# A two-layer hybrid decoder step on one core: another order of features in the output projections, row scores behind a merge, and later norms

## The chip, the core and the metric

The kernel runs on one core of one Trainium2 chip. The core has a matrix engine (TensorE; PE in the profile, its weight loads are PEld), a vector engine (VectorE, DVE), an activation engine (ScalarE, ACT), a general engine (GpSimd, POOL) and SyncE (SP), which issues the DMAs. SBUF is the on-chip memory, PSUM holds what matmuls sum up. The metric is the device time of one execution in microseconds.

## The reference: what is computed

One inference step of a trunk with two layers, for a prompt of 1024 tokens and 8 sample streams of 8 tokens each, 1024 features wide, in float32:

```python
for l in range(DEPTH):                                   # 2 layers
    if l < N_A_LAYERS:                                   # layer 0
        q, k, v, gate, qm = retention_inputs(xp, w_in_a[l], pos_p)
        o, st = retention_prompt(q, k, v, log_g)
        mix_p = concatenate([retention_output(o, gate), memory_attention(qm, mkv_p)])
    else:                                                # layer 1
        for g, (window, _) in enumerate(DIL_PAIRS):      # (128,1) (512,4) (2048,16)
            o, lse = dilated_prompt(q_p[:, :, hs], kv_p[:, :, 0, hs], kv_p[:, :, 1, hs], window, dil)
        mix_p = concatenate([combine_groups(outs_p, lses_p), memory_attention(qm_p, mkv_p)])
    xp = deepnorm_residual(xp, mix_p @ w_out[l], ln_mix_g[l], ln_mix_b[l])
    xp = deepnorm_residual(xp, swiglu_ffn(xp, w_ffn_in[l], w_ffn_out[l]), ln_ffn_g[l], ln_ffn_b[l])
```

The sample tokens go through the same layers, with retention states and key/value caches as inputs. `deepnorm_residual(x, h)` is the layer norm of `ALPHA * x + h`. `combine_groups` weighs the outputs of the three window groups by the softmax of their log-sums.

## The kernel before

**Layout.** Features lie on the 128 partitions, in 8 tiles of 128 (`KT`); the 1088 tokens (1024 of the prompt, 64 of the samples) lie along the free axis. They go in three chunks, `CH` = columns 0 to 512, 512 to 768 and 768 to 1088; the last holds the samples. `xh` and `xl` are the residual stream split in two fp32r halves; `mx` is what a mixer computes and later the sum that is normed. A float32 product is three matmuls, `wl*xh`, `wh*xl`, `wh*xh` (L316 to L318, and L764 to L766 and L814 to L816 in the FFN). The weight halves are made on the way: ACT rounds `wh`, DVE or POOL subtracts `wl` (L149, L152; these two lines are helpers that record most copies and elementwise operations).

**Order of the work.** A main program issues the projections. Small jobs (attention of a tile, a merge, a norm) are generators in a queue (`Streams`). At certain places of a projection the main program calls `S.tick()`, and each active job takes a step: up to `S.window` jobs, `S.rate` steps per tick. A job's `yield n` keeps it back for n ticks, a `yield` of a condition until that holds (`wait`). `S.until(cond)` takes steps, with ticks but no projection, until the condition holds. Within a dense product the ticks come after the features in `S.at`: of `TK`, (1, 3, 5) for block 0 of the second output projection, (4,) for the other blocks of either. Behind all this, a planner of the framework lays out each engine's queue: what was issued earlier has priority, but an instruction whose operands and buffers are there can be placed ahead of an earlier one that is not ready. So the issue order is a wish, and the trace shows what became of it.

**Layer 0** (`layer_a`, about 60 to 510 us): six retention heads, each with projections V, K, Q and a gate; the gates of heads 4 and 5 come last (`LATE`). `retention` is a job of some steps per head and chunk; its last transposes are the tile `rot` (L1078), which wait for `on` (L1063), which needs the statistics of L1055.

**Layer 1** (`layer_b`, about 1390 to 1785 us): six units (window group, half of the heads), `UNITS = ((2,0), (1,0), (0,0), (2,1), (1,1), (0,1))`. Each projects V, K, Q and then adds jobs to the queue. For the groups 1 and 2 these are `row_scores` (scores of the sample queries against cached keys, on DVE: 16 steps, each with one or two loads of `kc`, one of `qb`, one multiply, L1419, and two sums, L1422), `caches`, eight `attend`, a `spill`, and `sample`, which needs the rows and holds a lock (`locked`) for the length of its run, so that the samples of the units go one after another. For group 0 there is a `local_chunk` per chunk, which attends and then merges the three groups into `mx` (transposes of `fe`, tile `mtr`, L1353) and sets `("merge", j, c)`; then `sample`, and `merge_sample(j)`, which needs the three samples of j and sets `("msamp", j)` (tile `smt`, L1503). The rows of the units run one after another too (key `"rows"`). Before the change rows(1,1) run from about 1723 to 1787 us.

**Output projection** (`out_proj`, both layers): `mix = mx @ w_out`. Block 0 is chunk 0, block 1 is chunks 1 and 2. For each of the 8 features, `mx` is split into halves and `mx` gets the residual back (`xh + xl`). The halves of the first two features of block 0, and of all of block 1, lie in slots; those of later features of block 0 overwrite `xh` and `xl` of features whose residual was already returned. Then for each of 8 columns `m` the product over k = 0 to 7 goes to a PSUM bank (`dbank`: pool `pd` with 3 banks; `bank`: 4 banks), and DVE adds it to `ALPHA * mx` (L692). Block 1 of layer 1 waits for all merges, `("caches", 0, j)` and `("msamp", j)`.

**Norms** (`norm`): sums over the features, a matmul with `onesinv` for the mean (`lnm`, L599), subtraction, squares, a matmul for the variance (`lnv`, L619), its root on POOL (`lnr`), a matmul that spreads it (`lnb`, L630), and scale and shift. `LNY` gives the ticks before `lnm`, between `lnm` and `lnv`, and between `lnv` and `lnb`: the first triple for chunk 0 after the mixer, the second for the `calm` norms (chunks 1 and 2 after the mixer, chunk 0 after the FFN), the third for chunks 1 and 2 after the FFN. A calm norm first stands back by `LAZY` ticks, as do the outputs of chunk 0 in the last block (`y_out`). `combine_x` makes the inputs of the FFN from the normed chunks; the FFN's block 0 needs chunk 0, its block 1 the others.

**FFN** (`ffn`): two blocks of 512 and 576 tokens, 22 tiles of the hidden width in 6 groups; a tile is seven products (each 12 matmuls, then a tick), and after a group the output weights are applied.

Of the kernel before, what the change touches and what calls it, by code (L numbers as in the profile page):

```python
# [9 lines left out]
F32R = mybir.dt.float32r  # L10
# [4 lines left out]
P = 128  # L15
D = 1024
KT = 8
# [70 lines left out]
def trunk(ctx: ExitStack, tc: tile.TileContext, A: dict, O: dict, g128, g8):  # L88
# [13 lines left out]
    mm = nc.tensor.matmul  # L102
    dma = nc.sync.dma_start
    S = Streams(3)
    LNY = ((1, 5, 2), (3, 11, 5), (4, 7, 2))
    LAZY = (14, 14)
    RT = (2.3, 3.0, 1.0, 4.25, 4.25, 2.5)
    LAST = (((1,), (2,)), ((2,), (1,)))
    TK = ((3,), (2, 5), (1, 3, 5), (4,))
# [8 lines left out]
    def wait(*keys):  # L118
        if not all(k in done for k in keys):
            yield lambda: all(k in done for k in keys)  # L120
# [9 lines left out]
    def slot(shape, dt=F32, name="slot"):  # L130
        return slots.tile(shape, dt, tag="slot", name=name)
# [4 lines left out]
    def bank(name="bank"):  # L136
        return pa.tile([P, 512], F32, tag="pa", name=name)

    def dbank(name="pd"):
        return pd.tile([P, 512], F32, tag="pd", name=name)  # L140
# [10 lines left out]
    def tt(out, a, b, op, eng=None):  # L151
        (eng or nc.vector).tensor_tensor(out=out, in0=a, in1=b, op=op)  # L152
# [147 lines left out]
    def weights(key, ahead=None, keep=False):  # L300

        assert plan[at["next"]][0] == key, (plan[at["next"]][0], key)
        at["next"] += 1
        if not keep:
            for w in held:
                w.clear()
            held.clear()
        held.append([piece(1), piece(PA[1] if ahead is None else ahead)])
        return held[-1]

    def dense(out, w, rhs, kt=KT):

        for k in range(kt):
            rh, rl = rhs(k)
            wh, wl = (t[:, k % 4, :] for t in w[k // 4])
            mm(out, lhsT=wl, rhs=rh, start=(k == 0), stop=False)  # L316
            mm(out, lhsT=wh, rhs=rl, start=False, stop=False)  # L317
            mm(out, lhsT=wh, rhs=rh, start=False, stop=(k == kt - 1))  # L318
            if k in S.at and kt == KT:
                S.tick()  # L320
# [340 lines left out]
    BLK = (((0, 512),), ((512, 256), (768, 320)))  # L661
    BCH = ((0,), (1, 2))

    def out_proj(l, ready):
        for blk in range(2):
            S.at = TK[2] if l and blk == 0 else TK[3]
            S.until(lambda: all(k in done for c in BCH[blk] for k in ready(c)), blk if l else 1)
            b0, bn = BLK[blk][0][0], sum(n for _, n in BLK[blk])
            bs = slice(b0, b0 + bn)
            parts = []  # L670
            for k in range(KT):
                if blk == 0 and k > 1:
                    h, lo = xh[:, k - 2, bs], xl[:, k - 2, bs]
                elif k % 2 == 0:
                    hs, ls = (slot([P, 2, bn], F32R, nm) for nm in ("mixh", "mixl"))
                    h, lo = hs[:, 0], ls[:, 0]
                else:
                    h, lo = hs[:, 1], ls[:, 1]
                acopy(h, mx[:, k, bs])
                tt(lo, mx[:, k, bs], h.bitcast(F32), ALU.subtract)  # L680
                parts.append((h, lo))
                tt(mx[:, k, bs], xhf[:, k, bs], xlf[:, k, bs], ALU.add, nc.gpsimd if blk else nc.vector)
            done.add(("moved", l, blk))
            sums = [None, None]
            for m in range(KT):
                w = weights(("wo", l, blk, m))
                for i, c in enumerate(BCH[blk]):
                    c0, n = CH[c]
                    ps = (bank("po") if blk and m % 2 else dbank())[:, :n]
                    dense(ps, w, lambda k: tuple(t[:, c0 - b0:c0 - b0 + n] for t in parts[k]))  # L690
                    y = mx[:, m, c0:c0 + n]
                    nc.vector.scalar_tensor_tensor(out=y, in0=y, scalar=ALPHA, in1=ps, op0=ALU.mult, op1=ALU.add)  # L692
                    if blk == 0:
                        sums[i] = stat_add(sums[i], m, c, nc.vector)
                    S.tick()
            for i, c in enumerate(BCH[blk]):
                S.add(norm(c, sums[i], 0, l), level=2)
            S.add(combine_x(l, blk), level=2)
# [465 lines left out]
    def layer_b():  # L1164
# [219 lines left out]
        def row_scores(gi, j, Qt):  # L1384
# [30 lines left out]
            nxt = load(0)  # L1415
            for i in range(16):
                (kc, qb), nxt = nxt, load(i + 1) if i < 15 else None
                yield SR[i % 2]
                tt(qb, qb, bc(kc, 2, [P, 2, 2, P]), ALU.mult)  # L1419
                b, hf = i // 2, slice(i % 2 * 2, i % 2 * 2 + 2)  # L1420
                for h in range(2):
                    nc.vector.tensor_reduce(out=s5[:, hf, b, h, :], in_=qb[:, :, :, h * 64:(h + 1) * 64], op=ALU.add, axis=AX.X)  # L1422
# [141 lines left out]
    S.add(locked(mem_sample(0)))  # L1564
    layer_a()
    S.rate = RT[2]
    out_proj(0, lambda c: [("ret", h, c) for h in range(NRH)] + [("memT", 0, T) for T in range(8)] + [("mems", 0)])
    ffn(0, background)
    S.until(lambda: ("ln", 1, 0, 1) in done and ("ln", 1, 0, 2) in done and ("xparts", 0) in done)
    S.rate, S.at, S.window = RT[3], TK[1], WIN_[0]  # L1570
    layer_b()
    S.rate, S.window = RT[4], WIN_[1]
    out_proj(1, lambda c: [("merge", j, c) for j in range(2)] + [k for j in range(2) for k in (("caches", 0, j), ("msamp", j)) if c == 2])
    S.rate, S.window = RT[5], 3
    ffn(1, background)
    S.until(lambda: not S.q)
# [99 lines left out]
```

## Time and profile before

| what | time |
| --- | --- |
| median of 3 runs | 2707.31 us (2706.66 to 2708.17) |
| the profiled execution | 2703.15 us |
| its span, first to last instruction | 2701.3 us |
| PE busy in it | 2606.2 us |
| DVE, ACT, POOL busy | 1821.3, 1200.6, 933.4 us |
| mean granted clock of TensorE | 0.990 |

The profile is of one execution, and its times add up to that execution's time, not to the median. Busy times are unions of the instructions of an engine; PE's instructions are pipelined, so a busy PE need not be at its peak. In a timeline row stand the start, the length, the engine, the line, the operation, out<-in with the program's names, the shapes and the count, and in brackets how long the engine was idle before it and which instruction's end released it. In a view of stages each engine has its busy time and in brackets its count of instructions, then come the granted clock, the share of the DMA engines' time, and the rate in GB/s.

### The profile page before, as it was taken

How to read it: one execution, taken by the hardware profiler on the slowest of the kernel's cores; microseconds unless marked ns; L12 is line 12 of the kernel's file. 1: busy time of each engine (PE TensorE's matmuls, PEld its weight loads, DVE VectorE, ACT ScalarE, POOL GpSimd, SP SyncE). 2: the span in 40 equal slices, each digit the busy share in tenths (PEclk: the TensorE clock that was granted, in tenths of full speed). 3: DMA queues.
4: the chain of work that ended last, by engine and by line, in shares of the span. 5: the costliest groups of instructions: out<-in, count | busy, mean ns of one | idle time of the engine just before them, and what ended most of it. 6: DMA issues, size and time to landing. Idle time of an engine off the chain costs nothing. (4 is left out here: it accounts for less than half of the span.)

```text
span 2701.3 us, 48271 instructions
## 1 busy us (share of the span) xinstructions
PE 2606.2 (96%) x18057; PEld 2360.9 (87%) x18057; DVE 1821.3 (67%) x3843; ACT 1200.6 (44%) x2617; POOL 933.4 (35%) x1118
## 2 busy tenths in 40 slices
PE   8999999999999999999999999989999999999997
PEld 8778888798999989999977777768989998899997
DVE  4534345578777798666684775777987768866666
ACT  4432223344544554444455555544454445344434
POOL 0012223654444443333530111136444444433335
PEclk9999999999999999999999999999999999999998
DMA  7131111134333333332322553552324433433332
GB/s 252 32 95 51 54 48 56 58 93 132 113 113 112 125 100 106 121 103 89 116 91 87 159 163 91 157 148 87 102 91 133 125 119 121 133 114 114 98 96 84
DMA packets 417818, 289.22 MB, mean 107 GB/s; under 512 B 21360, under 2 KB 403120, under 8 KB 415920
## 3 DMA queue, kind: packets, MB, share of 16 engines
q1 hardware_dynamic: 417584, 286.13, 34.4%
q8 instruction: 143, 2.34, 0.4%
q14 instruction: 91, 0.75, 0.1%
HBM read 272.25 MB, written 40.83 MB: 116 GB/s over the span
## 5 line engine op out<-in xcount | busy, mean ns | idle before, releaser
L152 POOL TENSOR_TENSOR wl<-rawu,wh 128x256 fp32r<-128x256 f32 (+1 forms) x560 | 449.7, 827 | 834.1 <-ACT wh L149 748.6
L149 ACT ACTIVATE wh<-raw 128x512 fp32r<-128x512 f32 (+1 forms) x628 | 388.8, 623 | 569.7 <-DVE raw L152 200.2
L316 PE MATMUL pd<-xh,wl 128*128 128x512 f32 (+2 forms) x1200 | 419.4, 350 | 0.8 <-DVE t L439 0.7
L152 DVE TENSOR_TENSOR wl<-raw,wh 128x512 fp32r<-128x512 f32 x460 | 341.8, 747 | 115.3 <-ACT wh L149 111.4
L317 PE MATMUL pd<-xl,wh 128*128 128x512 f32 (+2 forms) x1200 | 407.7, 340 | 0.2 <-DVE xl L152 0.2
L318 PE MATMUL pd<-xh,wh 128*128 128x512 f32 (+2 forms) x1200 | 406.9, 340 | 0.0
L764 PE MATMUL gb<-xh,wl 128*128 128x256 f32 (+1 forms) x1232 | 357.4, 290 | 7.1 <-DVE up L152 3.3
L766 PE MATMUL gb<-xh,wh 128*128 128x256 f32 (+1 forms) x1232 | 356.4, 289 | 0.0
L765 PE MATMUL gb<-xl,wh 128*128 128x256 f32 (+1 forms) x1232 | 353.8, 287 | 0.0
L152 POOL TENSOR_TENSOR wl<-raw,wh 128x256 fp32r<-128x256 f32 x336 | 270.5, 830 | 120.9 <-ACT wh L149 105.5
L764 PE MATMUL pd<-xh,wl 128*128 128x256 f32 (+1 forms) x880 | 255.3, 290 | 7.9 <-DVE up L152 3.9
L149 ACT ACTIVATE wh<-rawu 128x512 fp32r<-128x512 f32 (+1 forms) x280 | 170.9, 614 | 198.9 <-PE pd L816 70.5
L316 PEld LDWEIGHTS pd<-xh,wl 128*128 128x128 f32 x1200 | 227.3, 190 | 36.1 <-issue 16.3
L766 PE MATMUL pd<-xh,wh 128*128 128x256 f32 (+1 forms) x880 | 254.1, 289 | 0.0
L765 PE MATMUL pd<-xl,wh 128*128 128x256 f32 (+1 forms) x880 | 252.1, 286 | 0.0
L317 PEld LDWEIGHTS pd<-xl,wh 128*128 128x128 f32 x1200 | 227.8, 190 | 25.2 <-issue 7.5
L318 PEld LDWEIGHTS pd<-xh,wh 128*128 128x128 f32 x1200 | 227.3, 189 | 24.0 <-issue 5.1
L764 PEld LDWEIGHTS gb<-xh,wl 128*128 128x128 f32 x1232 | 232.7, 189 | 10.0 <-DVE wl L152 3.1
L765 PEld LDWEIGHTS gb<-xl,wh 128*128 128x128 f32 x1232 | 234.4, 190 | 0.6 <-DVE xl L152 0.2
L766 PEld LDWEIGHTS gb<-xh,wh 128*128 128x128 f32 x1232 | 232.4, 189 | 0.0
L814 PE MATMUL gb<-hid,wl 128*128 128x512 f32 (+2 forms) x528 | 174.0, 331 | 4.3 <-ACT hid L149 2.2
L764 PEld LDWEIGHTS pd<-xh,wl 128*128 128x128 f32 x880 | 165.6, 188 | 10.3 <-issue 4.6
(344 smaller groups left out, 6130.5 us busy)
## 6 DMA issues: line engine op xcount, KB each, us to landing
rawu<-in_w_ffn_in_dram SPq DMA_DIRECT2D x88, 512.0 KB
raw<-in_w_ffn_in_dram SPq DMA_DIRECT2D x88, 512.0 KB
raw<-in_w_out_dram SPq DMA_DIRECT2D x32, 512.0 KB
raw<-in_w_ffn_out_dram SPq DMA_DIRECT2D x32, 512.0 KB
rawu<-in_w_ffn_out_dram SPq DMA_DIRECT2D x32, 512.0 KB
out_wins_dram<-in_cache_win_kv_g_dram SPq DMA_DIRECT2D x64, 256.0 KB
qb<-scr_q SPq DMA_DIRECT2D x64, 256.0 KB
raw<-in_w_in_a_dram SPq DMA_DIRECT2D x26, 512.0 KB
```

What stands on the lines that cost most here:

```text
L149: nc.scalar.activation(out, in_, AF.Copy, scale=scale)
L152: (eng or nc.vector).tensor_tensor(out=out, in0=a, in1=b, op=op)
L316: mm(out, lhsT=wl, rhs=rh, start=(k == 0), stop=False)
L317: mm(out, lhsT=wh, rhs=rl, start=False, stop=False)
L318: mm(out, lhsT=wh, rhs=rh, start=False, stop=(k == kt - 1))
L764: mm(ps, lhsT=wl[:, k], rhs=XH[:, i, k], start=start and k == 0, stop=False, skip_group_check=True)
L765: mm(ps, lhsT=wh[:, k], rhs=XL[:, i, k], start=False, stop=False, skip_group_check=True)
L766: mm(ps, lhsT=wh[:, k], rhs=XH[:, i, k], start=False, stop=stop and k == 3, skip_group_check=True)
L814: mm(ps, lhsT=wl[:, k], rhs=hid[k][:, 0, ts_], start=first, stop=False)
```

## The change

`LNY` and `LAZY` get other numbers. `out_proj` takes the features in a given order, and asks for each feature by itself whether it is ready; in block 0 the last `late` of them may come later: the first two columns (layer 0) or the first (layer 1) are begun with the others, then `until` waits for the late ones. `row_scores` of the last unit but one, (1, 1), waits after its first two loads for the first merge of its half, `("merge", 1, 0)`.

```diff
-    LNY = ((1, 5, 2), (3, 11, 5), (4, 7, 2))
-    LAZY = (14, 14)
+    LNY = ((1, 9, 4), (3, 11, 5), (4, 9, 3))
+    LAZY = (40, 30)
...
-    def out_proj(l, ready):
+    def out_proj(l, ready, order, late):
...
-            S.until(lambda: all(k in done for c in BCH[blk] for k in ready(c)), blk if l else 1)
...
-            parts = []
-            for k in range(KT):
-                if blk == 0 and k > 1:
-                    h, lo = xh[:, k - 2, bs], xl[:, k - 2, bs]
...
+            parts, pair = [None] * KT, []
+
+            def mix(p):
+                k = order[p]
+                if blk == 0 and p > 1:
+                    h, lo = xh[:, order[p - 2], bs], xl[:, order[p - 2], bs]
+                else:
+                    if p % 2 == 0:
+                        pair[:] = [slot([P, 2, bn], F32R, nm) for nm in ("mixh", "mixl")]
+                    h, lo = (t[:, p % 2] for t in pair)
                 acopy(h, mx[:, k, bs])
                 tt(lo, mx[:, k, bs], h.bitcast(F32), ALU.subtract)
-                parts.append((h, lo))
+                parts[k] = (h, lo)
                 tt(mx[:, k, bs], xhf[:, k, bs], xlf[:, k, bs], ALU.add, nc.gpsimd if blk else nc.vector)
+
+            def some(ps, w, c, ps_):
+                c0, n = CH[c]
+                for p in ps_:
+                    k = order[p]
+                    rh, rl = (t[:, c0 - b0:c0 - b0 + n] for t in parts[k])
+                    wh, wl = (t[:, k % 4, :] for t in w[k // 4])
+                    mm(ps, lhsT=wl, rhs=rh, start=(p == 0), stop=False)
+                    mm(ps, lhsT=wh, rhs=rl, start=False, stop=False)
+                    mm(ps, lhsT=wh, rhs=rh, start=False, stop=(p == KT - 1))
+                    if p in S.at:
+                        S.tick()
+
+            begun = []
+            first = KT - late if blk == 0 else KT
+            need = lambda ks: [key for c in BCH[blk] for k in ks for key in ready(k, c)]
+            S.until(lambda: all(key in done for key in need(order[:first])), blk if l else 1)
+            for p in range(first):
+                mix(p)
+            if blk == 0:
+                for m in range(2 - l):
+                    w, ps = weights(("wo", l, blk, m), 0 if m == 0 and l == 0 else 2, m > 0), dbank()
+                    some(ps, w, 0, range(first))
+                    begun.append((w, ps))
+                S.until(lambda: all(key in done for key in need(order[first:])), blk if l else 1)
+                for p in range(first, KT):
+                    mix(p)
             done.add(("moved", l, blk))
             sums = [None, None]
             for m in range(KT):
-                w = weights(("wo", l, blk, m))
+                w = begun[m][0] if m < len(begun) else weights(("wo", l, blk, m))
                 for i, c in enumerate(BCH[blk]):
                     c0, n = CH[c]
-                    ps = (bank("po") if blk and m % 2 else dbank())[:, :n]
-                    dense(ps, w, lambda k: tuple(t[:, c0 - b0:c0 - b0 + n] for t in parts[k]))
+                    if m < len(begun):
+                        ps = begun[m][1]
+                        some(ps, w, c, range(first, KT))
+                    else:
+                        ps = (bank("po") if blk and m % 2 else dbank())[:, :n]
+                        some(ps, w, c, range(KT))
...
             for i in range(16):
                 (kc, qb), nxt = nxt, load(i + 1) if i < 15 else None
+                if (gi, j) == UNITS[-2]:
+                    yield from wait(("merge", j, 0))
                 yield SR[i % 2]
                 tt(qb, qb, bc(kc, 2, [P, 2, 2, P]), ALU.mult)
...
-    out_proj(0, lambda c: [("ret", h, c) for h in range(NRH)] + [("memT", 0, T) for T in range(8)] + [("mems", 0)])
+    out_proj(0, lambda k, c: [("ret", k, c)] if k < NRH else [("memT", 0, T) for T in range(8)] + [("mems", 0)], (6, 7, 0, 1, 2, 3, 4, 5), 1)
...
-    out_proj(1, lambda c: [("merge", j, c) for j in range(2)] + [k for j in range(2) for k in (("caches", 0, j), ("msamp", j)) if c == 2])
+    out_proj(1, lambda k, c: [("merge", k % 2, c)] + [k for k in (("caches", 0, k % 2), ("msamp", k % 2)) if c == 2] if k < 6 else [],
+             (6, 7, 0, 2, 4, 1, 3, 5), 3)
```

More of the change, by code (lines that the diff above doesn't have):

```diff
@@ L662, in trunk @@
     BCH = ((0,), (1, 2))
-    def out_proj(l, ready):
+    def out_proj(l, ready, order, late):
         for blk in range(2):
             S.at = TK[2] if l and blk == 0 else TK[3]
-            S.until(lambda: all(k in done for c in BCH[blk] for k in ready(c)), blk if l else 1)
             b0, bn = BLK[blk][0][0], sum(n for _, n in BLK[blk])
             bs = slice(b0, b0 + bn)
-            parts = []
-            for k in range(KT):
-                if blk == 0 and k > 1:
-                    h, lo = xh[:, k - 2, bs], xl[:, k - 2, bs]
-                elif k % 2 == 0:
-                    hs, ls = (slot([P, 2, bn], F32R, nm) for nm in ("mixh", "mixl"))
-                    h, lo = hs[:, 0], ls[:, 0]
-                else:
-                    h, lo = hs[:, 1], ls[:, 1]
+            parts, pair = [None] * KT, []
[3 more added lines that the diff above has]
+                    h, lo = xh[:, order[p - 2], bs], xl[:, order[p - 2], bs]
+                else:
+                    if p % 2 == 0:
+                        pair[:] = [slot([P, 2, bn], F32R, nm) for nm in ("mixh", "mixl")]
+                    h, lo = (t[:, p % 2] for t in pair)
```

## The prediction

> **What bounds the kernel now.** I read the page first, then the busy time of each engine by stage, then PE's timeline where a stage has idle time.
>
> ```profile
> span 2701.3 us, 48271 instructions
> ...
> PE 2606.2 (96%) x18057; PEld 2360.9 (87%) x18057; DVE 1821.3 (67%) x3843; ACT 1200.6 (44%) x2617; POOL 933.4 (35%) x1118
> ...
> PEclk9999999999999999999999999999999999999998
> ```
>
> PE is busy 96% of the span and the change adds or removes no matmul. It can only win back PE's idle 95 us, or the time in which PE ran at a half granted clock. The view by stage shows where both lie (PE busy is the second number, the clock the third from the end):
>
> ```profile
> core 0: us, PE busy (x) PEld busy (x) DVE busy (x) ACT busy (x) POOL busy (x), PEclk, DMA share, GB/s
> ...
> 500.00:615.00 115.00, 109.59 (x651) 99.55 (x652) 70.83 (x109) 41.37 (x72) 62.67 (x67) 0.97 0.28 84
> 615.00:960.00 345.00, 339.68 (x2380) 316.98 (x2379) 271.30 (x504) 171.19 (x350) 152.51 (x190) 1.00 0.38 120
> 960.00:1350.00 390.00, 382.99 (x2856) 378.89 (x2855) 280.46 (x524) 175.70 (x337) 154.64 (x189) 1.00 0.33 104
> ...
> 1723.00:1783.00 60.00, 57.08 (x432) 41.53 (x430) 41.77 (x135) 32.70 (x98) 13.48 (x16) 1.00 0.58 160
> 1783.00:1797.00 14.00, 9.07 (x30) 6.13 (x28) 13.01 (x31) 7.46 (x18) 6.47 (x6) 0.63 0.26 72
> 1797.00:1861.00 64.00, 62.85 (x381) 43.89 (x380) 44.59 (x114) 26.74 (x71) 33.55 (x37) 1.00 0.33 97
> 1861.00:1912.00 51.00, 48.95 (x342) 48.03 (x341) 42.75 (x58) 23.90 (x42) 31.45 (x31) 0.93 0.32 94
> 1912.00:1980.00 68.00, 59.13 (x431) 56.33 (x431) 58.50 (x108) 32.64 (x70) 29.42 (x34) 0.96 0.35 111
> 1980.00:2280.00 300.00, 297.94 (x2042) 276.87 (x2041) 226.62 (x414) 145.87 (x291) 124.38 (x159) 1.00 0.37 117
> 2280.00:2345.00 65.00, 56.89 (x406) 54.54 (x404) 60.77 (x108) 29.37 (x60) 30.97 (x32) 0.97 0.44 144
> 2345.00:2675.00 330.00, 329.75 (x2481) 329.53 (x2482) 210.62 (x414) 138.79 (x267) 123.91 (x168) 1.00 0.33 102
> ```
>
> A stage's loss is its length less PE's busy time, plus its length times the missing clock. The large ones are the start of the second output projection (1783 to 1797: 4.9 + 0.37 x 14 = 10.1 us), the start of the second FFN (1912 to 1980: 8.9 + 2.7 = 11.6), its change of block (2280 to 2345: 8.1 + 2.0 = 10.1) and the first output projection (5.4 + 3.5 = 8.9). In the first three DVE is far busier than elsewhere: 13.0 of 14 us, 58.5 of 68, 60.8 of 65. What PE waits for there:
>
> ```profile
> 503.47 1.09 PE L1078 MATMUL rot<-kmain,on 128*128 128x128 f32 x3 [3.69 <-DVE on L1063]
> ...
> 572.39 1.05 PE L619 MATMUL lnv<-kmain,lnsq 128*128 128x1 f32 x8 [1.79 <-DVE lnsq L152]
> ...
> 1368.91 0.58 PE L619 MATMUL lnv<-kmain,lnsq 128*128 128x1 f32 x4 [1.82 <-DVE lnsq L152]
> ...
> 1777.86 0.55 PE L333 MATMUL vtr<-kmain,vT 128*128 128x128 f32 x3 [2.10 <-ACT vT L149]
> ...
> 1786.72 0.77 PE L316 MATMUL pd<-mixh,wl 128*128 128x512 f32 x1 [2.58 <-DVE t L439]
> ...
> 1793.04 2.82 PE L1353 MATMUL mtr<-kmain,fe 128*128 128x128 f32 x12 [1.00 <-ACT fe L149]
> ...
> 1875.34 1.79 PE L619 MATMUL lnv<-kmain,lnsq 128*128 128x1 f32 x8 [1.88 <-DVE lnsq L152]
> ...
> 1955.39 0.70 PE L599 MATMUL lnm<-lnsum,kmain 128*128 128x256 f32 x2 [2.63 <-DVE lnsum L152]
> ```
>
> **The change, part by part.** The times are those of the profiled execution: 2703.15 us, of which 1.85 lie outside the span; it is 4.2 under the median of 2707.31.
>
> *Ready features first, layer 1.* At 1783 PE has nothing but feature 0 of three columns, since feature 1 needs the first merge of j = 1, whose transposes come at 1793. In the new order five features (6, 7, 0, 2, 4) need only what was finished long before.
>
> ```profile
> 1859.57 0.40 PE L316 MATMUL pd<-xh,wl 128*128 128x512 f32 x1
> ...
> 1860.27 0.40 PE L316 MATMUL pd<-xh,wl 128*128 128x512 f32 x1
> ```
>
> One feature (three matmuls) takes 0.70 us, so five features in the three `pd` banks are 10.5 us of work, about as long as the stretch from 1783 to 1793. The row scores that leave DVE (next part) also bring the merge forward, and with it the `vtr` wait. I take the stage's 10.1 and the 2.1 of 1777.86: **-12**. Bounds: -12 and, if only the begun column runs (3.5 us), -4.
>
> *Row scores of unit (1,1) wait for merge (1, 0).* What moves:
>
> ```profile
> L152 DVE TENSOR_TENSOR qb<-qb,kc 128x512 f32<-128x512 f32 x16 | 12.5, 783 | 5.7 <-DMA qb<-scr_q 5.7
> L1422 DVE TENSOR_REDUCE sT<-qb 128x4 f32<-128x256 f32 x32 | 12.2, 409 | 0.1
> ```
>
> 16 x 783 + 32 x 409 ns = 25.6 us of DVE and 32 loads on SP, out of 1723 to 1787 and into what was 1797 to 1861. DVE there has 44.6 of 64 us; about 8 of these (the mixing of block 0) fall earlier now, and the mixing of block 1 (about 9) later, so 28 + 26 = 54 of 64: it fits. The loads pass the `vc`, `rm` and `raw` loads on SP's queue; DMA share is 0.33 there against 0.58 where they leave, so I cost them at nothing.
>
> Queued behind the wait is a chain: rows(1,1), then sample(1,1), which holds the lock, then sample(0,1), then merge_sample(1), and only then the mixing of block 1, whose 576 columns hold the sample's. Counting the yields: before, rows(1,1) end in the ticks of unit (0,1), and merge_sample(1) falls 10 ticks before the last of block 0's. After, the rows need 24 ticks, sample(1,1) 13, sample(0,1) 11, merge_sample 1: 49 against the 30 that block 0 still has, so **19 ticks** come behind it, in an `until` that issues no projection. Their length is bounded by the same steps before:
>
> ```profile
> 1824.40 0.43 PE L1463 MATMUL stb<-kT,zz 128*32 128x128 f32 x8
> ...
> 1840.84 0.28 ACT L149 ACTIVATE osamp<-sob 128x128 f32<-128x128 f32 x1 [0.68 <-PE sob L1485]
> ...
> 1842.70 0.16 DVE L152 TENSOR_TENSOR fM<-osamp,smp 128x1 f32<-128x1 f32 x1 [0.56 <-PE smp L1494]
> ...
> 1860.97 0.28 PE L316 MATMUL pd<-mixh,wl 128*128 128x256 f32 x1
> ```
>
> From `stb` to `osamp` took 16.7 us at block 0's pace, and the whole of sample(0,1) and the merge of the samples some 24. An estimate without the pacing: 14 us for these, 60% (most of it was waiting: the first matmuls last 0.43, the copy 0.28), some 2 for what is left of sample(1,1), 1.5 for the first mixing. Off go 4 us in which PE can start features 6 and 7 of block 1 in five banks. PE stands 13.5 us, and the half clock behind it costs 2 to 3: **+16**. Bounds: 0 (the planner sees no data dependence on the merge and pulls the rows forward) and +38 (19 ticks at block 0's 64 us / 32 = 2.0, less those 4, plus 4 for the clock). I take 16 since little else asks for the engines in that stretch, so it isn't paced by the projection.
>
> *Norms later in their ticks (LNY).* `lnv` is issued 4 ticks later (block 0's norm) or 2 (last norm of layer 0), and the last part after 2 or 1 more. A tick of block 1 is 51 us / 32 = 1.6 us, so 3 to 6 us cover the waits of 1.79, 1.82 and 1.88.
>
> ```profile
> 1366.00:1376.00 10.00, 8.18 (x33) 6.26 (x32) 8.07 (x18) 2.15 (x6) 1.20 (x3) 0.83 0.19 54
> 1870.00:1880.00 10.00, 8.12 (x46) 7.89 (x45) 6.70 (x11) 2.26 (x5) 8.10 (x8) 0.77 0.19 57
> 1880.00:1890.00 10.00, 10.00 (x72) 10.00 (x72) 6.66 (x11) 6.07 (x11) 1.42 (x2) 0.89 0.17 52
> ```
>
> The lost clock behind two of them is 1.7 and 2.3 + 1.1 = 3.4 us; in all 10.6. What is late next is the FFN's first input (`combine_x`); by the ticks it is issued 9 ticks before block 1's end (15 before), so it stays covered. I take **-8**; bounds -10.6 and +3, should `combine_x` be late by two ticks.
> The Trainium skill ("TensorE: Matmul & The Clock Gate", "What's actually happening") has the clock halved after at least one idle window of about 3.4 us. By it a wait of 1.88 us costs no clock, and this part would be worth 5 us less. The trace disagrees: behind 1875.34 the clock is 0.77, then 0.89.
>
> *Postponed norms (LAZY).* 26 and 16 ticks later. In the second FFN 2042 matmuls in 298 us are 0.146 us each, 12 to a tick: 1.75 us, so 45 and 28 us. The norm that holds PE at 1955 goes to about 2000, where DVE is 76% busy (226.6 of 300); the last outputs' first tiles go from about 2318 to behind 2345, where it is 64% busy. The same DVE work returns there, so part of the waits does too. I take half of 11.6, **-6**, a third of 10.1, **-3**, and -1 each in the first FFN's blocks, which lose 5.3 and 7.0. Bounds: -20 and +4 together.
>
> *Ready features first, layer 0.*
>
> ```profile
> 495.58 4.34 DVE L152 TENSOR_TENSOR mx<-xh,xl 128x512 f32<-128x512 f32 x2
> ...
> 501.16 0.68 DVE L1055 BATCH_NORM_STATS2 rst<-ro 128x6 f32<-128x128 f32 x3
> ```
>
> PE's 3.69 us at 503 is DVE doing the mixing ahead of the last retention's statistics. In the new order the third mixing overwrites `xh[6]`, which gate(5) reads late, so the mixing starts later and the statistics may go first. The stage loses 3.5 in clock besides. I take **-4**; bounds -7 and +3 (the mixing is then what PE lacks).
>
> Sum: -12 + 16 - 8 - 11 (LAZY: -6 - 3 - 1 - 1) - 4 = -19. Every shift makes the planner place engines' work anew, and some waits will return elsewhere; for these I allow +4: **-15**, 2688 for an execution like the profiled one, **2692** against the median.
>
> **Rivals.**
> (a) *The chain of the samples is paced* as before, +38 in place of 16: -15 + 22 = +7, 2714. It makes the kernel measurably slower from a stall of about 32 us between the blocks, with 4 of clock. For it: before, the samples kept to their ticks (`osamp` comes 11 ticks and 20.1 us ahead of block 0's end, 1.8 a tick). Against: PE was saturated then. 0.12.
> (b) *The wait does not do what it says*: the rows have no data from the merge, the planner pulls them into DVE's idle time and no stall comes: -15 - 16 = -31, 2676. For it: mixing of block 0 ran at 495 though issued behind gate(5). Against: rows(1,1) kept to their ticks before, 16 steps over 60 us with DVE 30% idle. 0.2.
> (c) *Waits only move*: DVE's demand is the same in every FFN stage, so LNY and LAZY give nothing: -12 + 16 - 4 + 4 = +4, 2711. 0.2.
> The forecast (-6 to -25, 2682 to 2701) has 0.48.
>
> **The numbers.** Forecast and (b) are faster: 0.68; (c) 0.20; (a) slower 0.12. A measurement can tell about 0.2%, 5.4 us, from no change. The range takes in (c) and most of (b) and leaves out (a): 2670 to 2713.
>
> **What would show it.** PE without waits over 1 us from feature 0 to the first merge of j = 1, and clock 1.00 there; rows' `qb` behind that merge's transposes; a PE gap between the last 512-column and the first features 0 to 5 of block 1, ended by `mixl`, about 13 us (0: (b), over 30: (a)); no `lnv` wait over 1 us; `lnm` of the 256 columns some 45 us later, with a shorter wait. The prediction is wrong if the gap is there and the FFN stages keep their losses, or if `combine_x` comes to hold the first matmuls of a FFN.

## The result, and the profile after

The changed kernel takes 2724.03 us (median of 4 runs, 2722.89 to 2724.57), the kernel before 2706.98 us on the same chip (4 runs, 2703.51 to 2708.17): a ratio of 1.0065, 95% interval 1.0047 to 1.0082. It is 17 us slower where I forecast 15 us faster, and lies outside my range of 2670 to 2713. The profiled execution took 2722.89 us, 19.7 more than that of before.

The page of the changed kernel, its span, PE's row of busy times and the granted clock in 40 slices:

```profile
span 2720.7 us, 48284 instructions
...
PE 2612.6 (96%) x18057; PEld 2366.7 (87%) x18057; DVE 1811.1 (67%) x3843; ACT 1200.5 (44%) x2617; POOL 929.6 (34%) x1118
...
PEclk9999999999999999999999999989999999999998
```

The matmuls are the same 18057, and PE is busy 6 us more, at a lower clock: one slice (the 27th, from about 1768 to 1836 us) has lost a tenth. To find the place, I cut each execution at matmuls of PE's timeline: A, B, D, E and F end at the first matmul of what follows, C and G at the last matmul of their hidden tiles, so that D also holds the rest of the first FFN's output products. The lengths are in us. Here are before, after and seven of the experiments told below (what each one is stands in its section):

| stage | before | after | e1 | e2 | e4 | e5 | e6 | e8 | e9 |
| --- | --- | --- | --- | --- | --- | --- | --- | --- | --- |
| A layer 0 and first projection | 614.4 | 609.7 | 609.6 | 608.6 | 616.3 | 611.7 | 611.3 | 608.0 | 607.5 |
| B first FFN, block 0 | 349.6 | 356.2 | 356.2 | 351.9 | 351.0 | 349.5 | 350.9 | 351.8 | 353.6 |
| C first FFN, block 1 | 377.1 | 373.2 | 373.2 | 373.1 | 377.2 | 377.2 | 373.1 | 373.1 | 373.2 |
| D layer 1, block 0 of second projection | 519.8 | 522.6 | 525.0 | 523.4 | 515.9 | 525.6 | 520.3 | 529.6 | 521.0 |
| E block 1 of second projection | 59.5 | 80.9 | 53.8 | 81.5 | 78.5 | 55.5 | 59.5 | 53.8 | 83.0 |
| F second FFN, block 0 | 358.6 | 364.5 | 362.9 | 363.0 | 358.5 | 358.8 | 357.8 | 357.3 | 358.1 |
| G second FFN, block 1 | 381.9 | 373.3 | 373.3 | 373.3 | 381.8 | 381.9 | 373.3 | 373.3 | 373.4 |
| last outputs | 40.4 | 40.4 | 40.9 | 40.4 | 40.4 | 40.4 | 40.9 | 40.7 | 40.4 |

C and G repeat to about 0.2 us between kernels that have the same code there (G is 381.8 to 381.9 with the old `LAZY[1]`, 373.3 to 373.4 with the new one, in every kernel), and so does E without the wait (53.8 or 59.5). B and F repeat to about 1.6 us, E with the wait to about 2 (80.9 to 83.0). A differs by up to 4 us, and D by much more: it is 525.0 in e1 and 536.5 in e3, which have the same code there. Why D does that is not shown, so a difference of a few us in one execution's D says little. From before to after: A -4.7, B +6.6, C -3.9, D +2.8, **E +21.4**, F +5.9, G -8.6: +19.5.

E is where the change lost most. The changed kernel's busy time by stretches, from the first matmul of the last 512-wide features to the start of the second FFN (columns as before: PE's busy time is the second number, the clock the third from the end):

```profile
1785.90:1861.60 75.70, 65.32 (x284) 46.41 (x283) 59.84 (x138) 25.84 (x64) 36.35 (x40) 0.89 0.47 141
1861.60:1875.00 13.40, 9.23 (x96) 6.90 (x94) 2.77 (x9) 2.65 (x7) 3.75 (x6) 1.00 0.66 193
1875.00:1886.40 11.40, 7.84 (x75) 5.44 (x76) 4.02 (x22) 2.97 (x10) 1.41 (x1) 0.85 0.34 95
1886.40:1915.00 28.60, 25.32 (x153) 23.92 (x152) 15.44 (x23) 10.35 (x19) 20.12 (x19) 0.82 0.28 84
```

From 1861.6 to 1886.4, 24.8 us, DVE, ACT and POOL are nearly idle too (6.8, 5.6 and 5.2 us): none of these engines is the limit, a chain is being waited for. PE's 17 us are only features 6 and 7, the end of the merges and the small matmuls of the samples. Then come 28.6 us at clock 0.82, which lose another 5.1. The chain is that of my prediction; PE's timeline shows its steps, and the first row is the merge that lets it go (line numbers behind `out_proj` are 33 to 35 higher than in the kernel before, so L1353 is now L1386):

```profile
1789.10 1.45 PE L1386 MATMUL mtr<-kmain,fe 128*128 128x128 f32 x8
...
1824.49 0.69 PE L1386 MATMUL mtr<-kmain,fe 128*128 128x128 f32 x2 [4.81 <-ACT fe L149]
...
1870.22 0.43 PE L1520 MATMUL sob<-vc,zz 128*32 128x128 f32 x8 [2.37 <-DMA vc<-in_cache_win_kv_g_dram]
...
1886.06 0.55 PE L1538 MATMUL smt<-kmain,smo 128*128 128x128 f32 x3 [1.85 <-DVE smo L1534]
1886.44 1.64 PE L599 MATMUL lnm<-lnsum,kmain 128*128 128x512 f32 x2
1887.09 1.20 PE L692 MATMUL po<-mixh,wl 128*128 128x256 f32 x1
...
1904.64 1.84 PE L619 MATMUL lnv<-kmain,lnsq 128*128 128x1 f32 x8 [3.16 <-DVE lnsq L152]
...
2023.52 1.24 PE L599 MATMUL lnm<-lnsum,kmain 128*128 128x256 f32 x4 [0.17 <-DVE lnsum L152]
...
2041.29 0.55 PE L797 MATMUL gb<-xh,wl 128*128 128x256 f32 x1 [10.09 <-DVE mx L152]
```

The merge comes at 1789, 4 us earlier than before, and PE does not wait long around it. But the rows stand in DVE's order among the factors of the next merge, and DVE waits for their loads:

```profile
1816.17 0.95 DVE L152 TENSOR_TENSOR qb<-qb,kc 128x512 f32<-128x512 f32 x1 [3.19 <-DMA qb<-scr_q]
```

PE then stands 4.81 us for that merge at 1824, and its clock is 0.50 from 1825 to 1835. `smt` comes 24.4 us after block 1's first matmul (1861.65), and the features 0 to 5 of block 1 (`po`) start behind it. The wait of `lnv` that LNY was to remove is there, longer than before. The last row is new: PE stands for 10.09 us in the second FFN, in a norm whose means (`lnm`, the row ahead of it) came without a wait. The row multiplies on DVE that stand behind the merge (the view of instructions by line; min/median/max in ns, first and last start):

```profile
L152 DVE TENSOR_TENSOR qb<-qb,kc x14: 673/692/1225, 1804.7 to 1852.4; 128x512 f32<-128x512 f32 x14
```

14 of the 16 are held back. The other two, whose loads are issued ahead of the wait, ran at 1729.09 and 1731.04: those the planner did pull forward, but no more, so rival (b) is out.

### The profile page after: what moved, and what is told of

It is laid out like the page before. It is cut to its first block, busy times and chain, and to the rows that moved or that the text cites. A ratio compares the mean times of both kernels' runs of the same rounds, so it can differ in the third digit from the quotient of the medians.

```text
span 2720.7 us, 48284 instructions
## 1 busy us (share of the span) xinstructions
PE 2612.6 (96%) x18057; PEld 2366.7 (87%) x18057; DVE 1811.1 (67%) x3843; ACT 1200.5 (44%) x2617; POOL 929.6 (34%) x1118
## 4 chain that ended last, share of the span: by engine, by line
PE 68%; DVE 10%; issue 5%; POOL 3%; DMA 2%; ACT 2%; SPq 1%; DVEq 0%; ACTq 0%; POOLq 0%
PE gb L799 5%; PE gb L797 5%; PE gb L798 5%; PE pd L797 4%; PE pd L799 4%; PE pd L798 3%; PE pd L316 3%; PE pd L317 3%; PE pd L318 3%; PE gb L847 3%; PE gb L848 3%; PE gb L849 3%; PE pd L847 3%; PE pd L848 3%; PE pd L849 3%
## 5 line engine op out<-in xcount | busy, mean ns | idle before, releaser
L316 PE MATMUL pd<-xh,wl 128*128 128x512 f32 (+2 forms) x1104 | 381.2, 346 | 1.8 <-ACT xh L149 1.0
L797 PE MATMUL gb<-xh,wl 128*128 128x256 f32 (+1 forms) x1232 | 357.4, 290 | 15.1 <-DVE mx L152 10.1
L317 PE MATMUL pd<-xl,wh 128*128 128x512 f32 (+2 forms) x1104 | 370.0, 336 | 0.0
L318 PE MATMUL pd<-xh,wh 128*128 128x512 f32 (+2 forms) x1104 | 369.3, 335 | 0.0
L316 PEld LDWEIGHTS pd<-xh,wl 128*128 128x128 f32 x1104 | 209.5, 190 | 32.0 <-issue 14.6
L317 PEld LDWEIGHTS pd<-xl,wh 128*128 128x128 f32 x1104 | 209.9, 190 | 22.1 <-issue 8.3
L318 PEld LDWEIGHTS pd<-xh,wh 128*128 128x128 f32 x1104 | 209.5, 190 | 18.9 <-issue 4.1
L847 PE MATMUL pd<-hid,wl 128*128 128x256 f32 (+2 forms) x509 | 168.4, 332 | 7.6 <-POOL wl L152 5.1
```

What stands on the lines that cost most here:

```text
L797: mm(ps, lhsT=wl[:, k], rhs=XH[:, i, k], start=start and k == 0, stop=False, skip_group_check=True)
L847: mm(ps, lhsT=wl[:, k], rhs=hid[k][:, 0, ts_], start=first, stop=False)
```

## The experiments

All were compared with the kernel before on the same chip (medians of 2707.98 us for e1 to e4, 2708.84 for e5 to e8, 2707.14 for e9 and e10, 2708.45 for e11). The ratios are with 95% intervals.

**e1: no wait for the merge.** The changed kernel without the added wait.

```diff
-                if (gi, j) == UNITS[-2]:
-                    yield from wait(("merge", j, 0))
```

> The changed kernel without the wait of the row scores; all else of the change stays. Theory T (the wait puts the chain of the samples behind block 0 and costs about 22 to 28 us): block 1 of the second output projection takes about 59 us again in place of 81, no PE wait of over 3 us between the blocks, time about 2698 (2692 to 2704). Rival R (the new order of the features and the begun columns hold up PE or the engines that feed it, the wait is innocent): stays at 2718 or more.

Measured: 2699.87 us (10 runs), ratio 0.9965 (0.9952 to 0.9979). The wait costs 24 us in the changed kernel; without it the rest of the change is a small gain. Its windows of the two blocks of the second projection:

```profile
1782.70:1864.00 81.30, 72.00 (x408) 50.49 (x407) 52.17 (x145) 33.80 (x87) 38.71 (x43) 0.94 0.31 91
1864.00:1917.80 53.80, 53.80 (x403) 53.32 (x402) 41.98 (x65) 24.04 (x44) 30.66 (x30) 1.00 0.31 90
```

Block 1 is now 53.8 us with PE busy throughout at full clock, 27.1 less than after. Block 0 is 81.3 us, 5.6 longer than after: that is all that the deferred rows had won.

**e4: the wait alone.** The kernel before with these two lines added.

```diff
+                if (gi, j) == UNITS[-2]:
+                    yield from wait(("merge", j, 0))
```

> The kernel before, with the wait of the row scores alone. Theory T: 2707 + 20 to 35, since the old order has not even features 6 and 7 first to fill the stall. Rival R: within 4 us of 2707.

Measured: 2721.19 us (7 runs), ratio 1.005 (1.0035 to 1.0066). The sign is right, the size is not: +13 against +20 to 35. Block 1 grew by 19.0 (59.5 to 78.5), and D shrank by 3.9. In the old order the wait may pay back more in block 0, but one execution's D is too uncertain to show it.

**e7: half the rows behind the merge.** The changed kernel in which only steps 8 to 15 wait.

```diff
-                if (gi, j) == UNITS[-2]:
+                if i >= 8 and (gi, j) == UNITS[-2]:
```

> The changed kernel, but only the last 8 of the 16 steps of the row scores wait for the merge. By the count of the yields merge_sample(1) then comes 7 ticks behind block 0 in place of 19. Theory T (the stall is the chain of the samples that is late): block 1 of the second projection takes 54 + 27 x 7/19 = 64 us (60 to 68) in place of 81, time about 2707. Rival (the stall comes from any wait at all, through what the planner makes of it, or from the late rows' load on DVE): 75 us or more, or no change in the time.

Measured: 2704.1 us (9 runs), ratio 0.9986 (0.9975 to 0.9998). Block 1 is 65.7 us, between e1's 53.8 and after's 80.9: half the rows give 44% of the cost in E, and D is 517.4, 5 us less than after. The forecast from the count of ticks was 64 us, so the cost goes with the length of the chain behind the merge. The late rows' own load on DVE is halved too, and this run alone does not tell the two apart; but in the changed kernel DVE is nearly idle in the stretch behind 1861.6.

**e11: the value loads on another queue.** In the trace's chain of waits of the changed kernel, the value loads of sample(1,1) hold the largest pieces; seven of them are issued behind a weight load that holds SP's queue until 1865.4 (start, length, what):

```profile
1865.38 0.37 SPq L229
1865.75 0.04 issue
1865.85 4.33 DMA vc<-in_cache_win_kv_g_dram
...
1870.35 5.18 DMA vc<-in_cache_win_kv_g_dram
```

So I had ACT issue them.

```diff
         t = rt([P, 4, P], name)
+        dma = nc.scalar.dma_start if (gi, j, name) == (1, 1, "vc") else nc.sync.dma_start
```

> The changed kernel with the value loads (vc) of sample(1,1) issued by ACT's DMA queue in place of SP's; all else as it was. Theory V (what made the chain behind block 0 longer than my 17.5 us, 24.8 from 1861.6 to 1886.4, is SP's order: seven of the eight vc loads stand behind a weight load that waits for a buffer until 1865.4, ten us after the first was issued): they start some 7 us earlier, the waits of sob for vc (2.37, 0.33, 0.35 and 1.20 us) go or shrink to under 1 us in all, the second block of the second projection falls from 80.8 us to 72 to 75, and the time is 2715 to 2718 us. Rival W (the loads are limited by free buffers or by the DMA's rate, or the chain by its ticks, so the queue doesn't matter): block 1 stays within 2 us of 80.8 and the time at 2721 to 2727 us.

Measured: 2721.79 us (4 runs), ratio 1.0044 (1.0028 to 1.0061); block 1 is 81.0 us. So rival W has the numbers, though the move did less than theory V needs. The seven loads were issued at 1864.57, only 1.3 us earlier (2.3 measured from block 1's first matmul) and not the 7 that I wanted, since ACT had work of its own ahead of them. PE's timeline of e11 shows them arrive late all the same:

```profile
1870.93 0.43 PE L1521 MATMUL sob<-vc,zz 128*32 128x128 f32 x8 [0.77 <-DMA vc<-in_cache_win_kv_g_dram]
1874.09 0.55 PE L1521 MATMUL sob<-vc,zz 128*32 128x128 f32 x8 [2.73 <-DMA vc<-in_cache_win_kv_g_dram]
```

Why is in two windows, the first of the changed kernel (the DMA engines' share and GB/s are the last two numbers):

```profile
1866.00:1875.60 9.60, 5.28 (x72) 3.34 (x70) 0.38 (x2) 0.31 (x1) 0.48 (x2) 1.00 0.99 292
```

and the second of e11:

```profile
1867.00:1875.00 8.00, 4.35 (x53) 2.94 (x57) 0.38 (x2) 0.88 (x2) 0.48 (x2) 0.95 0.89 260
```

In both the DMA engines are all but full, so another issuer does not make the loads shorter. The Trainium skill says so ("DMA: Bandwidth & Descriptors", "Issuing engines are not separate DMA queues"): the queues of the engines run on the same 16 DMA engines, and issuing from several saves only the time that the issuing takes. The runs agree as far as they go: the last of the seven landed 12.1 us into block 1 in place of 13.9, and `smt` came 24.5 us into it, against 24.4. The rest of the chain took up what was won. I had read a position in a chain as its cause.

**e5: the order alone.** The kernel before with the new `out_proj` (both orders, `late` 1 and 3), without the wait and with the old LNY and LAZY. Against the changed kernel:

```diff
-    LNY = ((1, 9, 4), (3, 11, 5), (4, 9, 3))
-    LAZY = (40, 30)
+    LNY = ((1, 5, 2), (3, 11, 5), (4, 7, 2))
+    LAZY = (14, 14)
...
-                if (gi, j) == UNITS[-2]:
-                    yield from wait(("merge", j, 0))
```

> The kernel before with the new out_proj alone (both orders and the begun columns; no wait, old LNY and LAZY). The prediction's step (ready features fill PE at 1783, worth 12 us in layer 1, and 4 in layer 0): 2708 - 16 = 2692. Theory D (DVE sets the pace there: the five early mixings, some 7 us of DVE, go ahead of the merge, which comes 5 to 9 us later): block 0 of the second projection ends no earlier than before against its start of the layer, only layer 0's 3 us are won, time about 2704 (2700 to 2709).

Measured: 2705.59 us (9 runs), ratio 0.9989 (0.9979 to 0.9998). The start of the second projection loses as much as before. First the kernel before, up to its first merge of j = 1:

```profile
1783.20:1793.00 9.80, 4.91 (x12) 2.63 (x11) 9.37 (x26) 5.24 (x15) 5.92 (x6) 0.68 0.35 97
```

Then e5, up to the same merge:

```profile
1781.90:1799.90 18.00, 13.20 (x47) 9.42 (x45) 15.20 (x36) 7.21 (x17) 8.17 (x6) 0.81 0.17 48
```

Before, 4.9 + 0.32 x 9.8 = 8.0 us are lost; in e5 4.8 + 0.19 x 18 = 8.2. PE has its ready features and runs 47 matmuls in place of 12, but the merge comes at 1799.9, not at 1793.0. DVE's timelines show why. Before, the merge's factors are ready for their reciprocal 8.7 us into the block:

```profile
1791.86 0.20 DVE L1377 RECIPROCAL fden<-fden 128x8 f32<-128x8 f32 x1
```

In e5 the mixing of the early features stands ahead of them, and it takes 16.8 us:

```profile
1787.66 0.69 DVE L152 TENSOR_TENSOR mixl<-mx,mixh 128x512 fp32r<-128x512 f32 x1
...
1792.09 1.28 DVE L152 TENSOR_TENSOR mx<-xh,xl 128x512 f32<-128x512 f32 x2
...
1798.72 0.20 DVE L1410 RECIPROCAL fden<-fden 128x8 f32<-128x8 f32 x1
...
1800.60 1.88 DVE L152 TENSOR_TENSOR mx<-mx,mtr 128x512 f32<-128x512 f32 x3 [1.32 <-PE mtr L1386]
```

**e2: the first number of LAZY back.** The changed kernel with one line altered.

```diff
-    LAZY = (40, 30)
+    LAZY = (14, 30)
```

> The changed kernel with LAZY[0] = 14 again (LAZY[1] stays 30). Theory T (the postponed norm of chunks 1 and 2 meets a stretch where it costs more, some 6 us in each FFN): the waits of 4.4 us (first FFN) and 10.1 us (second FFN) go, time about 2712 (2706 to 2717). Rival (the norm costs the same wherever it stands): within 3 us of 2724.

Measured: 2718.46 us (10 runs), ratio 1.0032 (1.0016 to 1.0048), 5.6 us under the changed kernel and between the two forecasts. So standing back by 40 in place of 14 costs; the stages say where: B 356.2 to 351.9 and F 364.5 to 363.0, 5.8 in all, though F's part is within its scatter. The wait of 10.1 us in F is gone, but F hardly gains: its first quarter of hidden tiles, where the norm stands again, grows from 78.5 to 97.6 us as the second falls from 99.3 to 78.8.

**e9: one tile later.** The changed kernel's 10.09 us, in DVE's timeline:

```profile
2035.11 0.48 DVE L152 TENSOR_TENSOR lnsq<-lnsq,sqt 128x256 f32<-128x256 f32 x1 [0.45 <-ACT sqt L609]
2035.52 0.42 DVE L152 TENSOR_TENSOR gp<-v,gp 128x256 f32<-128x256 f32 x1
2038.46 0.49 DVE L152 TENSOR_TENSOR lnsq<-lnsq,sqt 128x320 f32<-128x320 f32 x1 [2.53 <-ACT sqt L609]
...
2040.47 0.68 DVE L152 TENSOR_TENSOR mx<-mx,lnm 128x512 f32<-128x512 f32 x1
```

Both calm norms run at once. Their means (`lnm`) lie in two of the four PSUM banks of pool `pa`, and a tile of kind `gb` needs those four. A bank comes free with the last subtraction `mx<-mx,lnm` of its chunk. That of the 256 columns, at 2040.47, is what lets PE go at 2041.29; in DVE's order it stands behind sums of squares that wait for ACT. The tiles alternate between `pa` and the pool `pd`; so a shift by one tile (7 ticks) should put the norms beside a tile that does not need these banks.

```diff
-    LAZY = (40, 30)
+    LAZY = (47, 30)
```

> The changed kernel with LAZY = (47, 30): the calm norms after the mixer start 7 ticks, one hidden tile, later than with 40. Theory P (the two PSUM banks in which the means lie, pool pa, are what the next tile of kind gb lacks; PE's 10.1 us at 2041 are that, and a shift by one tile puts the squares beside a tile of kind pd, which does not need these banks): the wait of 10.1 us is gone or under 4 us, the second quarter of block 0's hidden tiles falls from 99.3 us to about 90, and the time is 2714 to 2718 us. Theory Q (it is only DVE's load: two norms of 576 columns at once in a stage where DVE is already full, wherever they are put): a wait of 6 us or more ended by DVE stays, and the time is 2720 to 2727 us.

Measured: 2719.39 us (10 runs), ratio 1.0041 (1.0029 to 1.0053). The long wait is gone; what is left at that place in PE's timeline of e9 is

```profile
2032.46 0.39 PE L797 MATMUL pd<-xh,wl 128*128 128x256 f32 x1 [1.88 <-DVE wl L152]
```

and F fell from 364.5 to 358.1, B from 356.2 to 353.6. The second quarter of F's hidden tiles is 91.5 us, near the 90 of theory P. In B a wait of the same kind is left (2.73 us at 710.18, a `gb` behind `mx`). The median fell by 4.6 only, between the two forecasts; the profiled execution was the fastest of the ten (2711.94). So the wait in F is explained, and about half of the time that I had put on it.

**e10: the same on the best version.** e8 (below) with the norms after the mixer as late as in e9.

```diff
-    LAZY = (14, 30)
+    LAZY = (47, 30)
```

> The best version so far (order of layer 0, new LNY, LAZY = (14, 30), no wait for rows, old order of layer 1; 2689.1 us) with LAZY = (47, 30). Theory P: the first quarters of block 0 gain 7 us each as they did with 40, and little of it comes back in the second, so 2680 to 2687 us. Theory Q: the second quarters give it all back and more, 2692 to 2697 us, about 6 above LAZY[0] = 14. If both come to within 2 us of 2689, the time of these norms is worth nothing either way.

Measured: 2694.84 us (5 runs), ratio 0.9954 (0.9939 to 0.997), against 0.9928 (0.9913 to 0.9942) for e8. As with 40, the first quarters of the hidden tiles gain (8.8 us in B and 13.7 in F) and the second quarters give it back (9.6 and 14.1): B is 353.4 against 351.8, F 357.7 against 357.3. Standing back further moves the norms' cost and saves nothing, as theory Q had it. The rest is in A (3.3) and D (1.6), which have the same code in both and scatter as much, so that these norms cost 5 us by standing back is not shown.

**e3: neither wait nor late norms.** The changed kernel with the edits of e1 and e2 together.

```diff
-    LAZY = (40, 30)
+    LAZY = (14, 30)
...
-                if (gi, j) == UNITS[-2]:
-                    yield from wait(("merge", j, 0))
```

> The changed kernel without the wait and with LAZY[0] = 14: what is left are the order of the features, LNY and LAZY[1]. If the two losses add up: about 2686 (2680 to 2693), faster than before by some 0.7%. If they overlap (the norm's late place only costs behind the stalled projection): as the first of these runs.

Measured: 2697.85 us (7 runs), ratio 0.996 (0.9946 to 0.9974), 2 us under e1. The two losses did not add up: in e1 going back is worth 2, in the changed kernel 5.6. In its profile, of the slowest of the seven (2703.13), D took 536.5 us, 11.5 more than e1's, which eats what B gave (4.4). Why D does that I did not find.

**e6 and e8: the parts that pay.** e6 has of the change only the order of layer 0 and the second number of LAZY. Against e5:

```diff
-    LAZY = (14, 14)
+    LAZY = (14, 30)
...
-             (6, 7, 0, 2, 4, 1, 3, 5), 3)
+             (0, 1, 2, 3, 4, 5, 6, 7), 0)
```

> The parts that won in the stage tables, alone: the order of layer 0 with its two begun columns, and LAZY[1] = 30. Layer 1 keeps the order 0 to 7 and waits for all features; no wait of the rows; LNY and LAZY[0] as before. If the parts add up: 3 to 4 (first projection) + 4 to 6 (first FFN, block 1) + 8 to 9 (second FFN, block 1) = 15 to 19 less than before, 2691 (2687 to 2696). If the early waits only move: 2700 or more.

Measured: 2689.76 us (4 runs), ratio 0.994 (0.9916 to 0.9964). C and G have the whole gain of the changed kernel (4.0 and 8.6 against before), A has 3.1, and only B gives 1.3 back, which is within its scatter. e8 is e6 with the new LNY:

```diff
-    LNY = ((1, 5, 2), (3, 11, 5), (4, 7, 2))
+    LNY = ((1, 9, 4), (3, 11, 5), (4, 9, 3))
```

> As the kernel with layer 0's order and LAZY[1] alone, with the new LNY besides. The prediction's step (LNY worth 8): 8 less than that kernel. Theory (LNY takes the waits out of block 1 of the projections, 2 and 5 us, but gives back 2 and 4 in the first quarter of the FFN behind each, and wins 1 to 3 at the end of layer 0): within 4 us of that kernel.

Measured: 2689.14 us (4 runs), ratio 0.9928 (0.9913 to 0.9942). Of the kernels here, e6 and e8 are the fastest. The two medians are 0.6 us apart, but their intervals leave some 7 us either way, so the time alone does not quite exclude the 8 of LNY. PE's timeline of e6

```profile
1870.00 1.64 PE L619 MATMUL lnv<-kmain,lnsq 128*128 128x1 f32 x8 [1.88 <-DVE lnsq L152]
```

and of e8:

```profile
1362.94 0.78 PE L599 MATMUL lnm<-lnsum,kmain 128*128 128x320 f32 x2 [1.69 <-DVE lnsum L152]
...
1881.32 0.95 PE L619 MATMUL lnv<-kmain,lnsq 128*128 128x1 f32 x8
```

The wait of `lnv` in block 1 is gone; in the last norm of layer 0 one of `lnm` has taken its place. Block 1 (E) falls from 59.5 to 53.8, and A by 3.3. But D grows from 520.3 to 529.6 in the same pair, as much as the other two give, and within D's scatter.

**The order of layer 1 once more.** e3 and e8 differ in one thing, the order of the features in layer 1 and its `late` columns: 2697.85 us with the new order, 2689.14 with the old one (ratios 0.996 and 0.9928, intervals apart). So beside the new LNY the new order costs about 9 us. D is 6.9 longer with it, within its scatter, but F is 363.2 against 357.3, beyond its scatter, and all of that lies in the first quarter of the hidden tiles (97.8 against 91.9 us). Beside the old LNY the order cost less (e5: F 358.8). Why F depends on it is not shown.

## Why the prediction was wrong

The steps as I put them, and what the runs showed. A difference of stages is between two profiled executions, one of time between medians.

| step | predicted | shown | by |
| --- | --- | --- | --- |
| ready features first, layer 1 | -12 | +1 | e5 against e6, D + E (+9 beside the new LNY: time of e3 against e8) |
| rows wait for the merge | +16 | +24 (D -2.4, E +27.1) | after against e1 |
| LNY | -8 | -1, some 7 either way | time of e8 against e6 |
| LAZY, first number | -6 - 1 | +6 | after against e2 (+2 without the wait: e1 against e3) |
| LAZY, second number | -3 - 1 | -12.6 | C and G of e6 against before |
| ready features first, layer 0 | -4 | -3 | A of e6 against before |
| waits that return | +4 | in the rows above | |
| sum | -15 | +15 | time: +17 |

The rows of this table were measured in different company, and that their sum comes so near the time is partly luck: LAZY's first number, LNY and the order of layer 1 cost other amounts beside other parts. Five of the runs form a path on which each differs from the next by one part: from before to e6 -19.1 us, then LNY -0.6 (e8), the order of layer 1 +8.7 (e3), LAZY's first number +2.0 (e1), and the wait +24.2 (after). On this path the wait is most of what was lost. (The medians of the kernel before differ by up to 1.9 us between these batches of runs.) Of the 32 us between my forecast and the time, the size of the wait has 8, the order of layer 1 has 13 to 21, LNY 7 and LAZY's first number 9 to 13; LAZY's second number gives 9 back.

**The mechanism of the wait was right, its size too small.** Chain, place and end were as predicted: a stretch between the blocks, ended when the samples are merged. I put 17.5 us on the 19 ticks behind block 0 (14 + 2 + 1.5); it took 24.8. Nor did it become the 38 of rival (a): 24.8 / 19 is 1.3 us a tick, between my 0.9 and its 2.0. I had costed the moved row loads at nothing because the DMA share was 0.33 in that block; it became 0.47, and DVE waited 3.19 us for one of them. The value loads of the samples, which move along, I had not counted at all. They come together at a share of 0.99, and PE waits for them:

```profile
PE sob L1520 <- DMA vc<-in_cache_win_kv_g_dram: 4.2, 4, 2.4
```

That is 4.2 us of the 24.8. Whether the chain would be shorter without these waits is not shown: in e11 the loads landed earlier and it was not. So the +16 was mis-sized, and what makes each tick 1.3 us stays open in part. After the stretch the half clock took 5.1 us, where I had 2 to 3, and `lnv` waited 3.16, which I had set to nothing in LNY.

**The step with the wrong reason is the -12.** I read in the profile that DVE was busy 13.0 of the 14 us in that stage, and then costed the new order by PE's work alone. The order takes nothing off DVE; it puts the mixing of five features ahead of the merge's factors on the engine that was full, and the merge moved from 1793 to 1800. I saw that the wait takes rows off DVE there, and that does help, but it belongs to the wait. Counted from the first matmul of block 0, the merge's transposes come after 9.9 us before and 10.6 in e6 and e8 (old order, no wait), 18.0 in e5 and 17.7 in e1 (new order, no wait), 4.3 in e4 (old order, wait) and 3.2 in the changed kernel (both). There the stretch up to the merge is as clean as I forecast; but block 0 loses it again further on, in the wait of 4.81 us at 1824 and the half clock behind it: 10.4 us idle and 0.11 x 75.7 = 8.3 of clock, against 6.1 and 5.4 before. Nor was DVE's load in these places as special as I wrote: it was 42.75 of 51 us in the row from 1861 to 1912 as well.

**LNY removed its waits of `lnv` where nothing else changed (e8), but the time hardly moved.** In the changed kernel the wait was back: `lnm` came only at 1886.44, at the end of the stall, where its squares shared DVE, ACT and POOL with the late mixing of features 0 to 5, and `lnv` came 18.2 us later (15.9 in e1). Rival (c), waits only move, describes this term well. Whether D's 9 us are LNY's is not shown: with the new LNY and no wait D was anything from 525.0 (e1) to 536.5 (e3), and without both 519.8 to 525.6.

**LAZY: one sign wrong, one size.** The norm of the second FFN moved as predicted: `lnm` comes 81 us into the stage where it came 35 us in before, and waits 0.17 us for DVE in place of 2.63. I counted DVE's share in the new place (76%) and asked no more of it. But a norm also holds PSUM banks as long as DVE is working on it, and two norms at once took half of a pool that the next tile needs whole. That is the 10.09 us of F in the changed kernel; B lost 4.3 us to the same number. The second number did far better than my third: the change of block had 10.1 us of loss, and 8.6 are won. The last outputs go to a stage where the spare DVE time was real: PE is busy 370.2 of G's 373 us now, 373.6 of 382 before.

**What the prediction's signs would have shown.** No long wait up to the first merge: right. `qb` behind that merge's transposes: right, but for two steps. `lnm` of the 256 columns some 45 us later with a shorter wait: right (46 us), but it brought no time. A gap ended by `mixl` of about 13 us: the place right, the gap spread over small waits among the samples' own matmuls, so that PE's busy time hid it. No `lnv` over 1 us: wrong. The chance of 0.12 for (a) was too small: I argued that nothing else asks for the engines there, and the chain was slow because of its own round trips and loads, not because of others.

## What to carry to other kernels

When a stage's bound is one engine (DVE here), a new order of work for another engine is worth only what it takes off the first; cost it there. A job put behind an event carries all its followers with it: count the chain to its last consumer and price its transfers at the rate they will have when they come together, not at the mean share of the stage. Before a job is put beside another stage, look at what it holds (PSUM banks, locks) as well as what it computes, and try the numbers of a combined change one by one: here two small parts gave 0.6% and the rest took it back twice over.

## What I had not expected of the hardware

The granted clock fell behind some short waits as behind longer ones, and stayed low after PE was busy again. In the changed kernel behind the wait of 10.09 us, up to 2041.29:

```profile
2031.00:2041.00 10.00, 0.20 (x2) 0.00 (x0) 6.18 (x14) 5.22 (x14) 6.77 (x9) 0.62 0.00 0
2041.00:2047.00 6.00, 5.71 (x27) 5.74 (x28) 5.95 (x14) 2.17 (x6) 0.00 (x0) 0.50 0.70 230
```

6 us of work at half clock cost 3 on top of the wait. In e9, behind a wait of 1.88 us:

```profile
2032.00:2037.00 5.00, 4.54 (x23) 4.43 (x24) 5.00 (x11) 1.70 (x4) 0.00 (x0) 0.66 0.34 108
```

So removing a wait of 2 us can be worth twice that, and a wait of 10 us costs 13. It need not be: behind the wait of 1.79 us at 572.39 in the kernel before, the clock stayed at 1.00:

```profile
572.00:582.00 10.00, 9.61 (x74) 9.61 (x75) 7.13 (x14) 4.23 (x7) 4.84 (x6) 1.00 0.36 107
```
